# Interleaving the segments of the first two r tiles in the RWKV layer's projections of a two-layer decoder step

## The chip, the cores and the metric

The kernel runs on one core of one Trainium2 chip. The metric is the device time of one execution in microseconds (us), taken on the chip; the median of several runs counts. A profile is one execution of the same program, with every instruction's start and duration on the core's engines: TensorE (PE; its weight loads are shown as PEld), VectorE (DVE), ScalarE (ACT), GpSimd (POOL) and SyncE (SP), which here only issues DMA transfers.

## What is computed

One inference step of a two-layer decoder. Layer 0 is a gated DeltaNet mixer, layer 1 an RWKV-7 mixer. 1104 token rows (64 sample tokens, 16 meta tokens, 1024 prompt tokens) run through both, with D = 1024. The change touches layer 1 only, of which this is the part that matters:

```python
xprev = jnp.concatenate([shift_prev[:, None], xn[:, :-1]], 1)
xx = xprev - xn
xs = xn[None] + xx[None] * mu[:, None, None, :]              # six mixed inputs
rkvz = jnp.einsum('sbtd,sde->sbte', xs[:4], w_rkvz)          # four 1024 x 1024 projections
r, k, v, z = rkvz[0], rkvz[1], rkvz[2], rkvz[3]
w = -jax.nn.softplus(-(w0 + jnp.tanh(xs[4] @ w1) @ w2)) - 0.5
a = jax.nn.sigmoid(a0 + (xs[5] @ a1) @ a2)
kk = l2norm((k * k_k).reshape(B, T, H, N))
decay = jnp.exp(-jnp.exp(w))
# then, token by token: S = S*decay - (S kk)(kk a)^T + v k^T ;  y = S r
```

The recurrence over tokens is computed in blocks of 64 tokens. Each block needs the inverse of a small triangular system, made from k, a and the decay alone; r, v and z are not needed for it.

## The kernel before

Tokens lie along the free dimension, in three segments of 384, 384 and 336 columns (`SEGS`). An output tile is 128 of the 1024 channels of one projection; each of its three segments is a sum of 24 matmuls: 8 pieces of the input dimension, each as high half of the weight times high half of x, low times high, and high times low (`dense_tile`, L1436). x and the weights are split into such halves (`split`, L135): ACT casts the high half (whi, or the high half of xa, xc, xh; L139), and POOL or DVE subtracts to give the low half (wlo, or the low half; L143). The tiles xa, xc, xh and xl hold the eight pieces of x in high and low halves.

In layer 1, `keys_decay_rate` (L1452) first makes k, the decays and a; their PE tiles are d and flora, and their results go to DRAM (kd, csd, ad). After it come the weights' opening (`projection_weights`, L2334), the mixed input of r (`mix`, L1290, with the temporaries mixs, three buffers; by segment, and in a segment piece by piece), and `projections` (L2370): 24 tiles, in the order r (m = 0), v (m = 2), z (m = 3), each with its segments in turn. Each tile's result is copied by ACT from PE's accumulator (d, L2494) and stored (rd for r, L2495).

A weight tile comes in two halves of 256 KB, numbered h: tile ti uses h = 2 ti for its first four pieces of x and 2 ti + 1 for the others. `fetch(h)` issues its load on SP's queue (wraw, two buffers), `cast(h)` splits it (whi and wlo, four buffers each). So a cast of h waits until PE has read the last matmul with h - 4, and a fetch of h until the split of h - 2 is done.

Inside `projections` the order is written by hand: PE's work is counted in half-tiles. After each half-tile (12 matmuls) `gap()` is called, which issues all that the list `plan` holds for that number, on all engines. The casts and fetches have such numbers, worked out from `starts`, the half-tile at which a tile begins. So do the openings of the recurrence's blocks, 24 items, one every three half-tiles: item n is loaded at about half-tile 3n + 1 (sldcs, slda, sldk, on SP) and begins at 3n + 4 (`system_steps`, L1566): on ACT two exponentials and a square (sal, sldcs, sqs), on DVE and POOL products (skk, sal, slda), and on PE the small matmuls frss and fL between half-tiles. Every fifth item is followed by the inverse on DVE (invtmp, invT) of the batch.

The part before `projections` (the opening of the weights, the mixing) is placed by the compiler's scheduler, which weaves it into the engines' queues beside the hand-made order; within one engine the queue is then strict. So mixing of r's x goes on beside the first tiles.

The lines of the loop that the change rewrites:

```python
for ti, (m, k) in enumerate(tiles):
    dst = {0: self.rd, 2: self.vd, 3: self.zd}[m]
    for s, (c0, n) in enumerate(SEGS[0:count(m, k)]):
```

Of the kernel before, what the change touches and what calls it, by code (L numbers as in the profile page):

```python
# [16 lines left out]
SEGS = [(0, 384), (384, 384), (768, 336)]  # L17
# [37 lines left out]
class Stream:  # L55
# [5 lines left out]
    def fetch(self):  # L61
        if self.fetched < len(self.srcs):
            w = self.raw[self.fetched] = self.b.t(self.b.wp, [128, 4, 128], "wraw", 2)
            v = self.srcs[self.fetched]
            m = v.shape[2]
            self.b.nc.sync.dma_start(w.rearrange("p a b -> p (a b)").rearrange("p (k m) -> p k m", m=m), v)
            self.fetched += 1

    def cast(self):
        if self.made < len(self.srcs):  # L70
            hi, lo = (self.b.t(self.b.wp, [128, 4, 128], n, self.b.WB, F32R) for n in ("whi", "wlo"))
            self.b.split(self.raw.pop(self.made), hi, lo)
            m = self.srcs[self.made].shape[2]
            self.w[self.made] = [x.rearrange("p a b -> p (a b)").rearrange("p (k m) -> p k m", m=m) for x in (hi, lo)]
            self.made += 1
# [13 lines left out]
class Builder:  # L89
# [8 lines left out]
    def t(self, pool, shape, tag, bufs=1, dt=F32):  # L98
        self.uid += 1
        return pool.tile(shape, dt, name=f"{tag}_{self.uid}", tag=tag, bufs=bufs)  # L100
# [2233 lines left out]
    def projection_weights(self):  # L2334

        nc, t = self.nc, self.t
        tiles = [(m, k) for m in (0, 2, 3) for k in range(8)]
        raw, whi, wlo = {}, {}, {}

        def fetch(h):  # L2340
            m, k = tiles[h // 2]
            v = self.i["rwkv_w_rkvz"][0, m][:, 128 * k:128 * k + 128].rearrange("(k p) m -> p k m", p=128)
            raw[h] = t(self.wp, [128, 4, 128], "wraw", 2)
            nc.sync.dma_start(raw[h], v[:, 4 * (h % 2):4 * (h % 2) + 4, :])

        def cast(h):
            whi[h], wlo[h] = (t(self.wp, [128, 4, 128], x, self.WB, F32R) for x in ("whi", "wlo"))
            self.split(raw.pop(h), whi[h], wlo[h])
        for h in (0, 1):
            fetch(h)  # L2350
        for h in (0, 1):
            cast(h)
            fetch(h + 2)
        cast(2)
        fetch(4)
        return tiles, whi, wlo, fetch, cast

    def late_weights(self):
# [11 lines left out]
    def projections(self, xa, xb, ip, opened, tiles, whi, wlo, fetch, cast):  # L2370
# [5 lines left out]
        count = lambda m, k: 3 if m == 3 and k >= self.ZK else len(segs[m])  # L2376
        plan = [[] for _ in range(180)]

        def put(g, f, late=2):
            plan[g].append((late, f))  # L2380
# [16 lines left out]
        starts, g = [], 0  # L2397
        for m, k in tiles:
            starts.append(g)
            g += 2 * count(m, k)  # L2400
        for h in range(3, 48):
            g = starts[h // 2]
            if h % 2 == 0:
                put(starts[h // 2 - 1] + 1, lambda h=h: cast(h), 1)
                put(starts[h // 2 - 1] + 3, lambda h=h: h + 2 < 48 and fetch(h + 2), 0)
            else:
                put(max(0, g - 1) if h > 3 else 5, lambda h=h: cast(h), 0)
                put(g + 1 if h > 3 else 7, lambda h=h: h + 2 < 48 and fetch(h + 2), 0)

        for m in (2, 3):  # L2410
            e, p0 = (48, 0) if m == 2 else (96, 48)
# [15 lines left out]
        for n in range(24):  # L2427
            B, g = batches[n // 5], g0(n)
# [12 lines left out]
        for B in batches:  # L2441
            g = g0(B.items[-1]) + 9
# [3 lines left out]
            g = at = max(at + 4, g + 2)  # L2446
# [4 lines left out]
            g = at + 4  # L2451
# [17 lines left out]
        g = starts[-1] + 2 * count(3, 7)  # L2469
# [10 lines left out]
            for x, f_ in sorted(self.plan.pop(at, []), key=lambda x: x[0]):  # L2480
                put(120 + 2 * u, f_, 4)

        for ti, (m, k) in enumerate(tiles):
            dst = {0: self.rd, 2: self.vd, 3: self.zd}[m]
            for s, (c0, n) in enumerate(SEGS[0:count(m, k)]):
                w = Halves(whi, 2 * ti), Halves(wlo, 2 * ti)
                p = self.dense_tile(w, zin if (m, s) == (3, 2) else xs[m], (0 if (m, s) == (3, 2) else c0, n), gap)

                def out(p=p, c0=c0, n=n, m=m, k=k, dst=dst):
                    f = t(self.ev, [128, 384], "ev", 3)  # L2490
                    if m == 3:
                        self.gate(f[:, 0:n], p[:, 0:n])
                    else:
                        nc.scalar.copy(f[:, 0:n], p[:, 0:n])  # L2494
                    put(now[0] + 2, lambda: nc.sync.dma_start(dst[k][:, c0:c0 + n], f[:, 0:n]))  # L2495
                put(now[0], out, 0)
# [130 lines left out]
```

## Time and profile before

| | us |
|---|---|
| median of 3 runs | 2273.2 |
| lowest and highest of them | 2270.88, 2274.19 |
| the profiled execution | 2271.01 |
| span of its trace | 2269.3 |

Times in the trace are counted from the span's start. Layer 1's opening weights (h = 0 on) are fetched from 1402.7 us on, and the stores of r go from 1448.0 to 1587.2 us. How to read the views: the page lists, for the whole execution, each engine's busy time and the chain that ended last, followed backwards from the last instruction to what released it. A timeline lists single instructions with their start, duration and, in brackets, the idle time of the engine ahead of them and what ended it. A window table gives the busy time of each engine in a stretch of the span, the granted clock of PE as a share of the full one, and the share of the DMA engines' time in use.

### The profile page before, as it was taken

The page shows a single profiled execution, that of the slowest core. Times are in us where ns is not written, and L with a number is a line of the kernel's source. Part 1 is how long each engine was busy: PE and PEld are TensorE (multiplying, and loading weights), DVE is VectorE, ACT ScalarE, POOL GpSimd, SP SyncE. Part 2 cuts the span into 40 slices and gives each one's busy share as a digit, 9 for nine tenths or more (in the row PEclk, how much of TensorE's full clock was granted, in tenths as well). Part 3 has the DMA queues.
Part 4 walks back from the last instruction along what each step waited for, and adds up shares of the span by engine and source line. Part 5 has one row for each costly group of instructions (what it writes and reads, how often), then busy time and mean ns, then how long its engine had stood idle before and what let it go on. Part 6 is the DMA issues. An engine that isn't in the chain of part 4 may idle for free.

```text
span 2269.3 us, 55274 instructions
## 1 busy us (share of the span) xinstructions
PE 2143.4 (94%) x20382; PEld 1966.5 (87%) x20382; DVE 1584.5 (70%) x4167; ACT 1250.7 (55%) x3631; POOL 1004.0 (44%) x1385
## 2 busy tenths in 40 slices
PE   7889999999999999989999999898999999999997
PEld 6788889889898989878999999798889977788886
DVE  6778788796969687885435762559887637667765
ACT  5536565556556565645433464644545456676763
POOL 4416262534335252614341442464543345566663
PEclk9999999999999999999999999999999999999997
DMA  3324242424333342436344234577786676655532
GB/s 113 79 67 127 65 124 67 110 80 109 85 105 99 81 122 71 114 78 184 95 143 106 70 103 169 167 237 196 206 247 155 157 186 155 173 162 158 168 118 91
DMA packets 495400, 291.61 MB, mean 129 GB/s; under 512 B 222345, under 2 KB 480506, under 8 KB 495130
## 3 DMA queue, kind: packets, MB, share of 16 engines
q1 hardware_dynamic: 495130, 288.08, 45.2%
q8 instruction: 161, 2.64, 0.5%
q14 instruction: 109, 0.89, 0.1%
HBM read 195.66 MB, written 92.30 MB: 127 GB/s over the span
## 4 chain that ended last, share of the span: by engine, by line
PE 46%; DVE 28%; issue 7%; ACT 6%; DMA 6%; POOL 3%; SPq 3%; DVEq 0%; POOLq 0%; ACTq 0%
PE d L129 10%; DVE invtmp L689 5%; PE rA L133 5%; DVE invT L691 5%; DVE cvy L634 4%; PE dz L129 4%; PE zo L129 3%; PE do L129 3%; PE rA L129 3%; PE dv L129 2%; PE fG L129 2%; PE dk L129 1%; DMA wraw<-in_gdn_w_out 1%; POOL wlo L143 1%; DVE E L765 1%
## 5 line engine op out<-in xcount | busy, mean ns | idle before, releaser
L143 POOL TENSOR_TENSOR wlo<-wraw,whi 128x512 fp32r<-128x512 f32 x238 | 321.1, 1350 | 490.1 <-ACT whi L139 391.5
L634 DVE SCALAR_TENSOR_TENSOR cvy<-raw,cw,cvy 128x408 f32<-128x408 f32 (+2 forms) x288 | 180.0, 625 | 35.8 <-ACT cvy L115 30.5
L689 DVE TENSOR_TENSOR invtmp<-invA,invT 72x31 f32<-72x31 f32 (+31 forms) x403 | 189.0, 469 | 15.6 <-POOL invT L678 10.1
L129 PE MATMUL d<-xc,whi 128*128 128x384 f32 (+1 forms) x640 | 181.4, 344 | 6.7 <-ACT xc L139 2.9
L691 DVE TENSOR_TENSOR invT<-invT,invtmp 72x31 f32<-72x31 f32 (+31 forms) x403 | 176.6, 438 | 14.1 <-DVE invtmp L689 0.2
L115 ACT ACTIVATE raw<-cvy 128x408 f32<-128x408 f32 (+2 forms) x96 | 49.8, 518 | 226.2 <-DVE cvy L634 178.0
L139 ACT CAST whi<-wraw 128x512 fp32r<-128x512 f32 x238 | 145.3, 612 | 26.0 <-DMA wraw<-in_rwkv_w_rkvz 12.5
L129 PE MATMUL dv<-xc,whi 128*128 128x384 f32 (+1 forms) x480 | 154.6, 343 | 0.0
L129 PE MATMUL dz<-xc,whi 128*128 128x384 f32 (+1 forms) x480 | 153.2, 342 | 0.0
L129 PEld LDWEIGHTS d<-xc,whi 128*128 128x128 f32 x640 | 118.0, 191 | 10.5 <-ACT xc L139 3.5
L129 PE MATMUL d<-xc,wlo 128*128 128x384 f32 (+1 forms) x320 | 105.4, 339 | 1.9 <-POOL wlo L143 1.8
L129 PE MATMUL d<-xa,whi 128*128 128x384 f32 (+1 forms) x336 | 101.2, 344 | 3.4 <-ACT whi L139 1.6
L129 PE MATMUL dz<-xa,whi 128*128 128x384 f32 (+1 forms) x288 | 102.3, 355 | 0.7 <-DVE zg L905 0.7
L129 PE MATMUL dv<-xa,whi 128*128 128x384 f32 (+1 forms) x288 | 100.9, 350 | 0.0
L1929 POOL TENSOR_SCALAR y<-y,mv,grs 128x64 f32<-128x64 f32 x132 | 81.1, 632 | 34.7 <-DVE grs L164 29.4
L129 PEld LDWEIGHTS dz<-xc,whi 128*128 128x128 f32 x480 | 90.4, 191 | 0.9
L129 PEld LDWEIGHTS dv<-xc,whi 128*128 128x128 f32 x480 | 89.0, 188 | 2.2 <-issue 1.6
L958 POOL TENSOR_SCALAR Sb<-Sb,eglb 128x128 f32<-128x128 f32 x128 | 90.4, 718 | 0.0
L160 POOL TENSOR_TENSOR ors<-ovar,cvals 128x6 f32<-128x6 f32 x24 | 35.8, 1492 | 118.9 <-DVE ovar L1121 118.6
L129 PE MATMUL d<-xl,whi 128*128 128x384 f32 (+1 forms) x256 | 82.8, 337 | 0.8 <-DVE xl L143 0.8
L129 PE MATMUL d<-xh,whi 128*128 128x384 f32 (+1 forms) x256 | 83.0, 336 | 0.1
L129 PE MATMUL d<-xh,wlo 128*128 128x384 f32 (+1 forms) x256 | 82.5, 336 | 0.0
(543 smaller groups left out, 7154.0 us busy)
## 6 DMA issues: line engine op xcount, KB each, us to landing
wraw<-in_gdn_w_in SPq DMA_DIRECT2D x96, 256.0 KB
wraw<-in_rwkv_w_rkvz SPq DMA_DIRECT2D x74, 256.0 KB
Sb<-in_state_gdn SPq DMA_DIRECT2D x64, 256.0 KB
wraw<-in_rwkv_w_o SPq DMA_DIRECT2D x48, 256.0 KB
E<-drow SPq DMA_DIRECT2D x24, 384.0 KB
attn<-drow SPq DMA_DIRECT2D x24, 384.0 KB
wraw<-in_gdn_w_out SPq DMA_DIRECT2D x36, 256.0 KB
out_s_gdn<-Sb SPq DMA_DIRECT2D x32, 256.0 KB
```

The source lines that it names most:

```text
L115: return self.nc.scalar.activation(out, in_, func, bias=bias, scale=scale, **kw)
L129: self.nc.tensor.matmul(out, lhsT, rhs, start=start, stop=stop)
L133: self.nc.tensor.matmul(out, lhsT, rhs, start=start, stop=True, skip_group_check=True)
L139: nc.scalar.copy(hi, x)
L143: e.tensor_tensor(lo, x, hi.bitcast(F32), op=ALU.subtract)
L160: self.nc.gpsimd.tensor_tensor(y, x, half.broadcast_to(sh), op=ALU.pow)
L634: nc.vector.scalar_tensor_tensor(ys[s][:, 0:wd(s)], raws[s][:, k:k + wd(s)], cw[k], ys[s][:, 0:wd(s)], op0=ALU.mult, op1=ALU.add)
L689: nc.vector.tensor_tensor(tmp, A[:, j, j + 1:32].unsqueeze(2).broadcast_to([nb, n, m]), Tv[:, j, 0:m].unsqueeze(1).broadcast_to([nb, n, m] ...
L691: nc.vector.tensor_tensor(Tv[:, j + 1:32, 0:m], Tv[:, j + 1:32, 0:m], tmp, op=ALU.subtract)
L765: nc.vector.scalar_tensor_tensor(E[:, tt, h], p_[s][:, 128 * tt:128 * tt + 128], c.bp[:, 3 * s + tt, h:h + 1], E[:, tt, h], op0=ALU.mult, ...
L958: nc.gpsimd.tensor_scalar(Sb[g][:, u], Sb[g][:, u], self.eglb[:, hv, 4 * g + u:4 * g + u + 1], None, op0=ALU.mult)
L1929: nc.gpsimd.tensor_scalar(y[:, q], y[:, q], mv[:, q, 0:1], P.rs[:, q:q + 1], op0=ALU.subtract, op1=ALU.mult)
```

## The change

The first two tiles (both of r) run by segments in turn: tile 0 and tile 1 with segment 0, both with segment 1, both with segment 2. From tile 2 on the order is as before. Casts of h = 0 to 3 (four buffers) all stand in the opening, with the fetches up to h = 5. Casts of h = 4 and 5 move from half-tiles 7 and 11 to 8 and 10, their fetches of h = 6 and 7 from 9 and 13 to 10 and 12.

```diff
         for h in (0, 1):
             fetch(h)
-        for h in (0, 1):
+        for h in range(4):
             cast(h)
             fetch(h + 2)
-        cast(2)
-        fetch(4)
         return tiles, whi, wlo, fetch, cast
...
-        for h in range(3, 48):
+        for h, g in ((4, 8), (5, 10)):
+            put(g, lambda h=h: cast(h), 1)
+            put(g + 2, lambda h=h: fetch(h + 2), 0)
+        for h in range(6, 48):
             g = starts[h // 2]
             if h % 2 == 0:
                 put(starts[h // 2 - 1] + 1, lambda h=h: cast(h), 1)
                 put(starts[h // 2 - 1] + 3, lambda h=h: h + 2 < 48 and fetch(h + 2), 0)
             else:
-                put(max(0, g - 1) if h > 3 else 5, lambda h=h: cast(h), 0)
-                put(g + 1 if h > 3 else 7, lambda h=h: h + 2 < 48 and fetch(h + 2), 0)
+                put(g - 1, lambda h=h: cast(h), 0)
+                put(g + 1, lambda h=h: h + 2 < 48 and fetch(h + 2), 0)
...
-        for ti, (m, k) in enumerate(tiles):
+        order = [(ti, s) for s in range(3) for ti in (0, 1)]
+        order += [(ti, s) for ti in range(2, 24) for s in range(count(*tiles[ti]))]
+        for ti, s in order:
+            m, k = tiles[ti]
             dst = {0: self.rd, 2: self.vd, 3: self.zd}[m]
-            for s, (c0, n) in enumerate(SEGS[0:count(m, k)]):
+            for c0, n in SEGS[s:s + 1]:
```

Each tile is numbered when it is made, so most numbers in the change are 6 higher for the same thing (the low-half weights and the mixed x keep their places in the rows). Lines from about L2400 on are 4 higher.

**PE, where tile 0's first segment ends.** whi_18275 and whi_18281 are the two high halves of tile 0's weight in both versions (h = 0 and 1), whi_18287 is that of tile 1 (h = 2). Before:

```order
L129 MATMUL flora_18256<-xa_100,lw2l_17144 128x336
L129 MATMUL d_18444<-xa_100,whi_18281 128x384
L129 MATMUL d_18475<-xa_100,whi_18275 128x384
L129 MATMUL d_18475<-xa_100,wlo_18276 128x384
L129 MATMUL d_18475<-xa_100,whi_18275 128x384 x2
```

In the change:

```order
L129 MATMUL flora_18256<-xa_100,lw2l_17144 128x336
L129 MATMUL d_18450<-xa_100,whi_18281 128x384
L129 MATMUL d_18481<-xa_100,whi_18287 128x384
L129 MATMUL d_18481<-xa_100,wlo_18288 128x384
L129 MATMUL d_18481<-xa_100,whi_18287 128x384 x2
```

The first segment is followed by tile 1's first instead of tile 0's second. Tile 0's third segment (128x336) comes after tile 1's second, d_18554, and after the recurrence's first fL; before, it stood two segments earlier:

```order
L129 MATMUL d_18554<-xa_100,whi_18293 128x384
L129 MATMUL d_18554<-xa_100,wlo_18294 128x384
L129 MATMUL d_18554<-xa_100,whi_18293 128x384
L129 MATMUL fL_18605<-skk_18529,sal_18530 64x64 x12
L129 MATMUL d_18630<-xa_100,whi_18275 128x336
L129 MATMUL d_18630<-xa_100,wlo_18276 128x336
```

**ACT, where the mixing of the third segment meets the recurrence's first item.** mixs rows of 128x336 are the third segment's mixing, casts from them make its pieces; ev<-d rows copy finished PE tiles; sal, sqs and sldcs belong to the items. Before:

```order
L2494 COPY ev_18521<-d_18475 128x384
L115 ACT_TABLE_LOAD
L115 ACTIVATE sal_18524<-sldcs_18469 128x383
L115 ACTIVATE sqs_18525<-sldk_18473,pcol_331 128x384
L139 CAST xc_104<-mixs_18399 128x336
L115 ACTIVATE mixs_18409<-xb_2582_14087,omu_520 128x336
L115 ACTIVATE sldcs_18469<-sldcs_18469 128x384
L139 CAST whi_18547<-wraw_18285 128x512
L139 CAST xc_104<-mixs_18404 128x336
L115 ACTIVATE mixs_18414<-xb_2583_14088,omu_520 128x336
L139 CAST xc_104<-mixs_18409 128x336
L139 CAST xh_2809_15429<-mixs_18414 128x336
```

In the change:

```order
L115 ACTIVATE sldcs_18475<-sldcs_18475 128x384
L115 ACTIVATE mixs_18415<-xb_2582_14087,omu_520 128x336
L139 CAST xc_104<-mixs_18410 128x336
L115 ACTIVATE mixs_18420<-xb_2583_14088,omu_520 128x336
L2498 COPY ev_18567<-d_18508 128x384
L139 CAST xc_104<-mixs_18415 128x336
L115 ACTIVATE sal_18620<-sldcs_18521 128x383
L115 ACTIVATE sqs_18621<-sldk_18525,pcol_331 128x384
L139 CAST xh_2809_15429<-mixs_18420 128x336
```

The cast of the weight half h = 3 (whi<-wraw) is gone from here; a copy of a PE tile (d_18508, tile 0's second segment) and the second item's sal and sqs now stand between the casts of the pieces. The weight's cast is found about 30 rows earlier, ahead of the cast of the first segment's last piece:

```order
L115 ACTIVATE mixs_18375<-xb_2582_14087,omu_520 128x384
L1433 COPY ev_18188<-d_18163 128x384
L139 CAST whi_18293<-wraw_18285 128x512
L139 CAST xa_100<-mixs_18348 128x384
L1433 COPY ev_18216<-d_18191 128x336
```

Before, the same rows stand there without the third.

**POOL, at the same place.** Rows from mixs make low halves of the pieces of x; skk and slda belong to the items. Before:

```order
L1583 TENSOR_TENSOR skk_18523<-skk_18523,sldcs_18469 128x384
L143 TENSOR_TENSOR wlo_18548<-wraw_18285,whi_18547 128x512
L1585 TENSOR_SCALAR slda_18471<-slda_18471,pcol_331,omka_83 128x384
L143 TENSOR_TENSOR xc_104<-mixs_18404,xc_104 128x336
L143 TENSOR_TENSOR xl_2810_15430<-mixs_18414,xh_2809_15429 128x336
L1592 TENSOR_TENSOR slda_18471<-slda_18471,sldk_18473 128x384
L143 TENSOR_TENSOR xa_100<-mixs_18424,xa_100 128x336
```

In the change:

```order
L1583 TENSOR_TENSOR skk_18529<-skk_18529,sldcs_18475 128x384
L1585 TENSOR_SCALAR slda_18477<-slda_18477,pcol_331,omka_83 128x384
L143 TENSOR_TENSOR xc_104<-mixs_18410,xc_104 128x336
L1592 TENSOR_TENSOR slda_18477<-slda_18477,sldk_18479 128x384
L1576 MEMSET sal_18620 128x6
L143 TENSOR_TENSOR xl_2810_15430<-mixs_18420,xh_2809_15429 128x336
L1578 MEMSET sal_18620 128x8
L1583 TENSOR_TENSOR skk_18619<-skk_18619,sldcs_18521 128x384
L143 TENSOR_TENSOR xa_100<-mixs_18430,xa_100 128x336
```

The weight's low half has left this place, the first item's second slda step stands ahead of xl, and the second item's skk ahead of the last piece (xa).

## The prediction

> **What bounds the kernel now.** I read the page's totals first: TensorE (PE) is the busiest engine and the largest share of the chain that ended last.
>
> ```profile
> PE 2143.4 (94%) x20382; PEld 1966.5 (87%) x20382; DVE 1584.5 (70%) x4167; ACT 1250.7 (55%) x3631; POOL 1004.0 (44%) x1385
> PE 46%; DVE 28%; issue 7%; ACT 6%; DMA 6%; POOL 3%; SPq 3%; DVEq 0%; POOLq 0%; ACTq 0%
> ```
>
> Then the stage that the diff touches, cut into stretches at tile edges (start and end in us, then busy us and count of each engine, the granted PE clock, DMA share, GB/s).
>
> ```profile
> core 0: us, PE busy (x) PEld busy (x) DVE busy (x) ACT busy (x) POOL busy (x), PEclk, DMA share, GB/s
> 1443.07:1447.40 4.33, 4.33 (x26) 4.33 (x27) 3.58 (x6) 3.31 (x9) 3.15 (x8) 1.00 0.59 205
> 1447.40:1461.66 14.26, 8.18 (x26) 5.75 (x25) 8.12 (x11) 8.88 (x18) 8.87 (x10) 0.67 0.55 177
> 1461.66:1478.07 16.41, 16.41 (x170) 15.30 (x168) 3.90 (x10) 5.11 (x11) 8.46 (x14) 0.98 0.50 159
> 1478.07:1520.90 42.83, 42.83 (x436) 39.78 (x434) 18.33 (x37) 18.67 (x41) 28.14 (x40) 1.00 0.81 238
> 1520.90:1620.00 99.10, 91.27 (x988) 83.58 (x988) 93.27 (x178) 49.84 (x112) 48.62 (x54) 0.97 0.69 198
> ```
>
> The first row is tile 0's second segment: 4.33 us, no gap. The second row is its third segment. It has fewer columns (336 for 384), yet takes 14.26 us; PE is busy for 8.18 of them, at two thirds of the clock. The third row is the whole of tile 1. The timeline of PE tells why (start, us, instruction, idle time before it and what ended it):
>
> ```profile
> 1442.89 0.62 PE L129 MATMUL d<-xa,whi 128*128 128x384 f32 x2 [0.66 <-POOL xa L143]
> ...
> 1448.30 0.42 PE L129 MATMUL d<-xa,whi 128*128 128x336 f32 x1
> 1451.34 0.42 PE L129 MATMUL d<-xc,whi 128*128 128x336 f32 x1 [2.62 <-ACT xc L139]
> ...
> 1452.21 0.65 PE L129 MATMUL d<-xc,whi 128*128 128x336 f32 x1 [0.29 <-DVE xc L143]
> 1453.11 0.65 PE L129 MATMUL d<-xc,whi 128*128 128x336 f32 x1 [0.25 <-ACT xc L139]
> ...
> 1456.87 0.93 PE L129 MATMUL d<-xc,whi 128*128 128x336 f32 x2 [2.83 <-POOL xc L143]
> ```
>
> The third segment waits for its own input, the mixed x (tiles xa, xc, xh, xl), piece by piece: 2.62 + 0.29 + 0.25 + 2.83 = 5.99 us of idle PE, and the rest at a low clock. The chain of waits confirms that the pieces set the pace here (start, us, what):
>
> ```profile
> 1452.26 1.23 POOL skk L1583
> 1453.49 1.23 POOL wlo L143
> 1454.71 0.93 POOL slda L1585
> 1455.64 0.28 issue
> 1455.93 0.89 POOL xc L143
> 1456.81 1.12 POOL xl L143
> 1457.94 1.23 POOL slda L1592
> 1459.16 0.91 issue
> 1460.12 0.90 POOL xa L143
> 1461.01 0.04 issue
> 1461.06 3.13 PE d L129 x13
> 1464.18 0.79 PE frss L129 x24
> 1464.98 2.29 PE d L129 x12
> 1467.27 0.84 PE fL L129 x24
> ...
> 1473.30 2.04 PE d L129 x12
> 1475.34 0.84 PE fL L129 x24
> 1476.18 4.14 PE d L129 x24
> ```
>
> Up to 1461 the chain lies on POOL (mixing, and the recurrence's skk and slda), after it on PE alone. So the stage waits for x once, and for about ten us.
>
> **The change, part by part.** *The order of the six segments.* Nothing is added or removed on PE; tile 1's first two segments and tile 0's second now stand ahead of tile 0's third. I rebuild PE's path from 1443.07, where tile 0's first segment ends in both versions. Prices: an unbroken 384-column segment 4.33 (first window row). Tile 1's middle segment is broken by the recurrence's matmuls: half of 4.33, frss 0.79, second half 2.29, fL 0.84, together 6.09. A 336-column segment: halves 2.04 and, from 1476.18 to the tile's edge at 1478.07, 1.89, so 3.93. Tile 1's third, with frss and fL: 0.79 + 2.04 + 0.84 + 1.89 = 5.56. Sum 4.33 + 4.33 + 6.09 + 3.93 + 5.56 = 24.2 us. Before, the same work runs from 1443.07 to 1478.07, 35.0 us. **If no piece of x is late, PE gains 10.8 us.** Of this 10.3 are the third segment's 14.26 - 3.93; the rest is the low clock at the head of tile 1.
>
> *Is x in time?* Tile 0's third segment now starts at 1443.07 + 4.33 + 4.33 + 6.09 = 1457.8 instead of 1447.4. It takes the eight pieces one after the other, about 0.49 us each (3.93 / 8), and the last one at about 1461.5. The pieces themselves keep their path, but POOL's queue differs: the low half of the weight (wlo, 1.23) leaves it, the next item's skk (1.23, taken like the first) comes in ahead of the last piece. From 1452.26: skk 1.23, slda 0.93, gap 0.28, xc 0.89 ends at 1455.6, where 1459.5 would do; slda 1.23 and xl 1.12 end at 1457.9, where 1460.8 would do; skk 1.23 and xa 0.90 end at 1460.1, where 1461.5 would do. The least slack is 1.4 us, before what follows.
>
> *The moved weight cast.* The fourth half (h = 3) is now split in the opening, some 16 us earlier on ACT, and so on POOL; the fetches of h = 5 and after move with it on SP's queue.
>
> ```profile
> 1439.20 0.58 ACT L115 ACTIVATE ev<-flora,pcol 128x384 f32<-128x384 f32 x1 [1.04 <-DMA kd<-ev]
> ...
> 1452.08 0.60 ACT L139 CAST whi<-wraw 128x512 fp32r<-128x512 f32 x1
> 1452.59 0.47 ACT L139 CAST xc<-mixs 128x336 fp32r<-128x336 f32 x1
> ```
>
> The cast costs ACT 0.51 (1452.08 to 1452.59). At its new place, about 1436, ACT has 1.04 us of idle time three microseconds later, where it waits for the landing of a kd store that leaves ahead of the cast. That hides it for the piece that tile 0's first segment waits for (1442.89). Without this cover the cost is 0.5. The scans and loads that hang on the ACT instruction between the two may slip by the same 0.5: the last piece then ends at 1460.6, slack 0.9. POOL's 1.23 falls in a stretch with POOL idle. SP waits there for POOL's split before it can refill that buffer; the csd stores stand behind it, but their scans start 1.5 us later anyway. I take nothing for all this, with 0 and 0.5 as ends.
>
> *The later casts.* h = 4 and 5 may be split only when tile 0's third segment has read its halves, at half-tiles 8 and 10. From the first, at about 1459.8, to tile 2's start at 1467.3 there are 7.5 us; cast and split take 0.6 and 1.23, behind at most the last piece. On ACT the eviction of the third segment and the cast of h = 5 stand behind that wait; neither is due before 1461.7. Nothing, unless POOL is 5 us behind.
>
> *SP's queue.* The loads of the recurrence's items now have less lead. Their stores, casts and evictions are the same in number.
>
> ```profile
> 1446.07 0.38 SPq L1554 DMA_DIRECT2D sldk<-kd  x1
> ...
> 1470.89 0.32 SPq L1554 DMA_DIRECT2D sldk<-kd  x1
> 1450.11 0.62 DVE L1580 SCALAR_TENSOR_TENSOR skk<-sldk,pcol,slda 128x384 f32<-128x384 f32 x1 [1.50 <-DMA sldk<-kd]
> ...
> 1481.90 0.62 DVE L1580 SCALAR_TENSOR_TENSOR skk<-sldk,pcol,slda 128x384 f32<-128x384 f32 x1
> ```
>
> The first two loads of 1446 are in use 4.0 us after issue (1450.11, a real wait). The fourth item's, issued at 1470.89, is used 11.0 us later. In the change I find it issued at about 1464.3, behind a weight fetch that waits for POOL's split of h = 4, and used at 1469.5 or later: lead 5.2 against 4.0. I take nothing; the ends are nothing and 2 us.
>
> *What comes after.* From tile 2 on, the order on every engine is the old one, and positions are counted in half-tiles. So all of it moves with PE, if nothing there is tied to another clock. The window from 1520.90 is VectorE's (93.27 of 99.1 us busy), yet the chain enters it from PE:
>
> ```profile
> 1520.93 0.82 PE frss L129 x24
> ...
> 1522.07 1.15 DVE skk L1580
> ```
>
> DVE is idle for more than half of the window before (18.33 of 42.83), so it carries no backlog into it. The gain is kept.
>
> **The sum.** The profiled execution took 2271.01 us; less 10.8 it is 2260.2. The median of the runs is 2273.2, 2.2 above it, so the forecast is **2262.4**.
>
> Two rules of the Trainium skill bear on this. The row at 1447.40 shows a clock of 0.67 around gaps of 2.62 and 2.83 us. The page "TensorE: Matmul & The Clock Gate", section "Part 1: The HAM clock gate", says that PE falls to half rate after an idle window of about 3.4 us, that these windows run free of the program, and that it stays there for at least one; the trace agrees in kind (gaps below 3.4 us were enough here), and by it the loss goes away with the gaps. POOL's slda took 0.93 above. The page "SBUF — State Buffer", section "SBUF: two separate sides", says that a VectorE operation with two SBUF inputs and a GpSimd operation lock each other out for a whole instruction; as the change crowds the same pieces and two items of the recurrence into these microseconds, it speaks against the slack: an estimate by it, one 0.62 us DVE operation ahead of each of three POOL operations, makes the last piece 1.9 us later and the gain about 1 us smaller.
>
> **The rivals.** *A smaller stall remains.* For it: slack of 0.9 to 1.4 us, three engines in strict queues, ACT copies of finished PE tiles now standing between the casts. Against it: the other pieces have 3 us. If the mixing slips by 4 us, PE waits 3, and loses about as much as half of the old clock loss (14.26 - 5.99 - 3.93 = 4.3, so 2): gain 5.8, 2267; by 2 us, 2264.
>
> *The gain is given back.* If the DMA queues (0.81 busy, 238 GB/s from 1478 to 1520) or VectorE after 1520 hold a pace of their own, PE arrives earlier and waits there: 2273. Against it: PE is busy in all of the 42.83 us and VectorE's first steps follow PE.
>
> *The low-clock spells move.* The window from 1520.90 has 0.97 of the clock: 99.1 x 0.03 / 0.5 is 6 us at half, which costs up to 3 us of PE. The gaps that cause it stand, but spells may fall otherwise after a shift: 2259 or 2266. (This is the page on the clock gate again, free-running windows.)
>
> *Slower.* The loads' lead: if a load of sldcs, slda or sldk takes 9 us instead of 4.0 while the weight fetch stands ahead of it, each of the first items holds ACT, and with it the eviction of PE's tiles, by some 4 us. Four items cost 16 us, more than the gain: 2278. It decides from a landing of about 5 us on, if several items are hit; a lead of 11 us returns once POOL has caught up, which speaks against four.
>
> That the change doesn't do what it says is out: PE's order has the third segment behind tile 1's second.
>
> **How the numbers follow.** Forecast 0.64; a smaller stall 0.14; given back 0.10; spells 0.06; slower 0.05; 0.01 is left. A measurement of this kernel can tell about 0.2% (4.5 us) from no change. Faster by more: forecast, smaller stall and spells, 0.84. Same: given back and the rest, 0.11. Slower 0.05. The range goes from the spells' good end, with a little for the edges, 2258.5, to the smaller stall's bad end, 2267.5.
>
> **What would show it.** Right: PE's row for tile 0's third segment without idle time, at about 1458 to 1462, 4 us long, clock near 1.00 in the whole stretch; tile 2 starting near 1467; the chain on PE from 1443 on, POOL's pieces gone from it; the windows after it as long as before. A smaller stall would show as "<-POOL xa" or "<-POOL xl" ahead of d near 1460. Given back: tile 2 early, but tile 8 or the end not. Slower: PE ahead of frss or fL waiting for sqs, skk, and ACT for sldk. The forecast is wrong if tile 2 starts after 1471, or if the end moves by less than tile 2 does.

## The result, and the profile after

| | before | the change |
|---|---|---|
| median, us | 2272.8 (4 runs) | 2259.3 (4 runs) |
| lowest and highest, us | 2270.88, 2274.19 | 2256.02, 2262.72 |
| profiled execution, us | 2271.01 | 2262.07 |
| span of its trace, us | 2269.3 | 2260.3 |

The ratio of the times is 0.994, with a 95% interval of 0.9922 to 0.9958: faster by 0.4 to 0.8%. The forecast was 2262.4 in a range from 2258.5 to 2267.5. The medians lie 13.5 us apart, more than the 10.8 that were forecast and than the 10.1 that the stage itself gives below. The interval (9.5 to 17.7 us) holds all three figures, and the two repeats give 11.5 and 12.1; whether some 2 us come from elsewhere, the runs do not show. All medians in this document leave out two executions that took far longer than the others of their kernel, 3993.51 us of the kernel before and 2864.16 us of a variant.

The page of the change, first the engines' busy times, then the shares of the chain that ended last:

```profile
PE 2142.3 (95%) x20382; PEld 1967.9 (87%) x20382; DVE 1581.5 (70%) x4167; ACT 1251.0 (55%) x3631; POOL 1005.7 (44%) x1385
PE 51%; DVE 26%; ACT 7%; issue 6%; DMA 6%; POOL 3%; SPq 1%; DVEq 0%; POOLq 0%; ACTq 0%
```

PE does the same matmuls (20382). Its share of the chain rose from 46% to 51%, that of the issue of DMAs on SP fell from 3% to 1%; these are totals of the whole span, and the windows of the stage say more. They are cut where the segments end, so each of the first five rows is one segment of the new order: tile 1's first, tile 0's second, tile 1's second (with frss and fL), tile 0's third, tile 1's third (with frss and fL). Columns as before.

```profile
1444.40:1448.74 4.34, 4.34 (x26) 4.34 (x27) 3.58 (x6) 3.32 (x9) 3.16 (x8) 1.00 0.63 210
1448.74:1453.10 4.36, 4.36 (x27) 4.36 (x26) 1.79 (x3) 4.07 (x8) 1.04 (x3) 1.00 0.78 237
1453.10:1459.00 5.90, 5.90 (x73) 5.33 (x71) 4.63 (x9) 5.11 (x12) 5.50 (x6) 1.00 0.40 136
1459.00:1463.67 4.67, 4.33 (x28) 3.70 (x25) 3.67 (x6) 1.85 (x4) 2.73 (x5) 1.00 0.61 211
1463.67:1469.30 5.63, 5.63 (x73) 5.35 (x73) 2.33 (x4) 2.30 (x5) 5.33 (x8) 1.00 0.59 164
1469.30:1512.40 43.10, 43.10 (x444) 40.06 (x444) 19.77 (x40) 18.86 (x42) 29.61 (x42) 1.00 0.90 265
1512.40:1611.40 99.00, 91.34 (x985) 83.65 (x983) 93.21 (x178) 49.95 (x113) 48.88 (x54) 0.97 0.69 197
```

The first five add up to 24.9 us, where the same matmuls took 35.0 before. PE is busy in all but 0.34 us of them, and the granted clock is 1.00 throughout. The third segment fell from 14.26 us at 0.67 of the clock to 4.67 us. The sixth and seventh row, 43.10 and 99.00 us, are what they were (42.83 and 99.10): the frss near which they are cut starts 42.79 us after tile 2 in both traces (1478.07 to 1520.86, and 1469.30 to 1512.09).

PE's timeline shows the one wait left, and that it stands where the prediction looked for it (start, us, instruction, idle before it and what ended that):

```profile
1444.22 0.62 PE L129 MATMUL d<-xa,whi 128*128 128x384 f32 x2 [0.78 <-POOL xa L143]
...
1463.32 0.42 PE L129 MATMUL d<-xa,whi 128*128 128x336 f32 x1 [0.34 <-POOL xa L143]
```

Between 1444.22 and 1463.32 no row of PE names a wait, frss at 1455.07 and fL at 1458.15 among them; at 1463.32 it waits 0.34 us for the last piece. The chain of waits around it (start, us, what):

```profile
1459.40 0.62 DVE skk L1580
1460.06 0.09 issue
1460.15 1.26 POOL skk L1583
1461.41 0.91 issue
1462.36 0.92 POOL xa L143
1463.28 0.04 issue
1463.32 0.42 PE d L129
1463.74 0.79 PE frss L129 x24
```

So the chain still runs through x up to 1463, though PE waits only 0.34 us for it. After that PE alone carries the chain through the stage.

Is the gain kept? One window from tile 2's first matmul to the end of the span, first of before, then of the change (this one begins 0.1 us behind tile 2's first matmul, which is at 1469.30):

```profile
1478.07:2269.30 791.23, 751.18 (x9626) 665.47 (x9624) 551.01 (x1463) 445.71 (x1276) 416.69 (x518) 0.97 0.62 172
```

```profile
1469.40:2260.30 790.90, 750.58 (x9625) 665.22 (x9623) 550.62 (x1465) 446.13 (x1276) 418.27 (x520) 0.97 0.62 173
```

From 1469.30 on it is 791.0 us, against 791.23 before: all of the gain reaches the end. The two spans differ by 9.0 us: 10.1 less from the end of tile 0's first segment to tile 2 (35.0 to 24.9), 0.2 less behind it, and 1.3 more ahead of it (1443.07 to 1444.40), where both kernels run the same matmuls.

### The profile page after: what moved, and what is told of

It is laid out like the page before. It is cut to its first block, busy times and chain, and to the rows that moved or that the text cites. A ratio compares the mean times of both kernels' runs of the same rounds, so it can differ in the third digit from the quotient of the medians.

```text
span 2260.3 us, 55274 instructions
## 1 busy us (share of the span) xinstructions
PE 2142.3 (95%) x20382; PEld 1967.9 (87%) x20382; DVE 1581.5 (70%) x4167; ACT 1251.0 (55%) x3631; POOL 1005.7 (44%) x1385
## 4 chain that ended last, share of the span: by engine, by line
PE 51%; DVE 26%; ACT 7%; issue 6%; DMA 6%; POOL 3%; SPq 1%; DVEq 0%; POOLq 0%; ACTq 0%
PE d L129 12%; PE rA L133 5%; PE dz L129 4%; PE do L129 4%; DVE invtmp L689 4%; DVE cvy L634 4%; DVE invT L691 4%; PE rA L129 3%; PE zo L129 3%; PE dv L129 3%; PE fG L129 2%; PE dk L129 2%; DMA wraw<-in_gdn_w_out 1%; PE zz L129 1%; DVE E L765 1%
## 5 line engine op out<-in xcount | busy, mean ns | idle before, releaser
L691 DVE TENSOR_TENSOR invT<-invT,invtmp 72x31 f32<-72x31 f32 (+31 forms) x403 | 176.9, 439 | 14.1 <-DVE invtmp L689 0.2
L139 ACT CAST whi<-wraw 128x512 fp32r<-128x512 f32 x238 | 145.4, 612 | 29.5 <-DMA wraw<-in_rwkv_w_rkvz 14.1
```

The lines of the kernel that those rows point to most:

```text
L139: nc.scalar.copy(hi, x)
L691: nc.vector.tensor_tensor(Tv[:, j + 1:32, 0:m], Tv[:, j + 1:32, 0:m], tmp, op=ALU.subtract)
```

## The experiments

The measure below is the time from the end of tile 0's first segment to tile 2's first matmul, the same work on PE in all kernels with these edges: 35.0 us before, 24.9 in the change. Its edges are good to some 0.2 us. The runs with one execution show the measure and the waits in one trace; their times alone could not tell a few us, as single executions of the kernel before went from 2264 to 2283. In four stretches of measurement the kernel before had medians of 2272.4, 2270.5, 2274.1 and 2270.5.

### The change again

No edit. It ran twice more, the second time beside a later experiment.

> The change once more, for its spread. My theory (tile 0's third segment waited for the pieces of its mixed x, and gets other PE work ahead of it now): tile 0's third segment lasts 4 to 5 us, tile 2 starts 10 us earlier after tile 0's first segment than before (25 instead of 35 us), and the rest follows unchanged, so the time is 9 to 14 us under the kernel before. The rival, that part of the 13.5 us between the medians comes from elsewhere than this stage: the traces differ by more than 2 us in a part that the change doesn't touch.

> The change again, unedited, to stand beside the run with the last piece on VectorE. Theory: 2257 to 2262, 0.4 to 0.7% below the kernel before; tile 2 starts 25 to 26 us after tile 0's first segment ends.

Medians 2260.98 (9 runs) and 2262.01 (6), ratios 0.9944 (0.9926 to 0.9963) and 0.9954 (0.9936 to 0.9972). The windows, first of one, then of the other, with their part behind tile 2:

```profile
1438.42:1463.97 25.55, 25.55 (x217) 24.49 (x218) 15.72 (x26) 16.73 (x36) 17.80 (x27) 0.94 0.56 179
1463.97:2259.40 795.43, 756.39 (x9626) 670.50 (x9624) 552.04 (x1465) 446.87 (x1276) 419.49 (x520) 0.96 0.62 173
```

```profile
1441.00:1465.33 24.33, 24.33 (x218) 23.22 (x219) 16.03 (x26) 16.55 (x36) 17.91 (x27) 1.00 0.61 192
1465.33:2257.40 792.07, 753.42 (x9625) 667.83 (x9623) 551.42 (x1465) 445.89 (x1276) 417.19 (x520) 0.97 0.62 173
```

In both PE is busy for the whole stretch: the 0.34 us wait is not in every execution. 24.33 is the predicted sum of 24.2 within 0.1, and below the 25 to 26 expected of the second repeat; the other lost 1.2 to a low clock (0.94). Both medians are as expected. Behind tile 2 the same program took 791.0, 792.1 and 795.4 us, with granted clocks of 0.97, 0.97 and 0.96: the clock's spells, as far as these traces show, move the time by some 4 us from one execution to the next. Ahead of the stage, too, the traces of one program lie up to 6 us apart (the first segment ends at 1444.4, 1438.4 and 1441.0). So the difference of more than 2 us in parts that the change does not touch, which the rival named, is there, but between executions of one program.

### Only the casts early

```diff
-        for h in (0, 1):
+        for h in range(4):
             cast(h)
             fetch(h + 2)
-        cast(2)
-        fetch(4)
```

The cast of h = 3 and the fetch of h = 5 leave the plan for it (half-tiles 5 and 7). The rest is the kernel before, with the old order of segments.

> The earlier casts alone, with the segments in the old order. My theory: the stall stays; at best the piece on POOL that PE waits for longest comes 1.2 us earlier, as the weight's low half has left the queue ahead of it. From the end of tile 0's first segment to tile 2's start 33.5 to 35 us (35.0 before, 24.9 with the change). The rival, that freeing POOL and ACT of the weight's split is the larger part of the gain: under 29 us.

Time 2269.91 (one run); the measure is 33.5 us. PE's timeline in the third segment:

```profile
1450.73 0.42 PE L129 MATMUL d<-xc,whi 128*128 128x336 f32 x1 [2.36 <-ACT xc L139]
1451.98 0.65 PE L129 MATMUL d<-xc,whi 128*128 128x336 f32 x1 [0.21 <-ACT xc L139]
1454.80 0.93 PE L129 MATMUL d<-xc,whi 128*128 128x336 f32 x2 [1.89 <-POOL xc L143]
1457.15 0.65 PE L129 MATMUL d<-xl,whi 128*128 128x336 f32 x1 [0.30 <-POOL xl L143]
```

The stall stays, 4.8 us of waits for 6.0. The early casts alone give 1.5 us, as the theory had it: the gain needs the order of the segments.

### Only the order, with the fourth cast late

```diff
-        for h in range(4):
+        for h in range(3):
             cast(h)
             fetch(h + 2)
...
-        for h, g in ((4, 8), (5, 10)):
+        for h, g in ((3, 2), (4, 8), (5, 10)):
```

> The change, with one part of it taken back: the cast of h = 3 is issued after half-tile 2 instead of in the opening, so the first segments of the two tiles run in turn while the fourth half of the weights is split beside them. Theory (the gain is PE's order of segments; where the cast of h = 3 stands is worth about its own 0.5 us on ACT and 1.2 us on POOL): tile 2 starts 25 to 27 us after tile 0's first segment ends (24.9 in the change, 35.0 before), with a wait of PE of at most 1.5 us for whi or wlo in tile 1's first segment. Rival (the opening's early casts are what makes the order possible): PE waits 3 us or more in tile 1's first segment, or the pieces of x end so much later that tile 2 starts 29 us or more after that point.

Time 2263.06 (one run); the measure is 28.6 us, between the two expectations: the wait, 0.23 + 2.21 us, is more than the theory allowed and less than the rival asked. POOL's timeline, and then PE's:

```profile
1441.57 1.60 POOL L143 TENSOR_TENSOR wlo<-wraw,whi 128x512 fp32r<-128x512 f32 x1
```

```profile
1440.58 0.44 PE L129 MATMUL d<-xc,whi 128*128 128x384 f32 x1 [0.23 <-ACT whi L139]
1443.22 0.44 PE L129 MATMUL d<-xc,wlo 128*128 128x384 f32 x1 [2.21 <-POOL wlo L143]
...
1444.43 0.52 PE L129 MATMUL d<-xh,wlo 128*128 128x384 f32 x1
1444.75 0.52 PE L129 MATMUL d<-xl,whi 128*128 128x384 f32 x1
...
1447.85 0.33 PE L129 MATMUL d<-xc,whi 128*128 128x384 f32 x1
```

The split of the weight stands on POOL behind other work and is late. 1.2 us after PE goes on, its matmuls stand 0.32 us apart instead of 0.17, for 3.42 us (1444.43 to 1447.85), which costs half of it, some 1.6 us. Waits 2.4 and clock 1.6 less the 0.34 of the change make the 3.7 us (28.6 - 24.9). So the early fourth cast is worth 3.7 us of the 10 between these two traces (3.1 and 4.3 against the two repeats of the change): it is part of the gain and not only a cost. The Trainium skill, "TensorE: Matmul & The Clock Gate", section "Part 1: The HAM clock gate", gives 3.4 us as the length of the gate's window; the spell of 3.42 agrees. The page asks for an idle window of that length ahead of the fall, but the longest gap here was only 2.21; the measurement decides.

### One segment later instead of two

```diff
-        order = [(ti, s) for s in range(3) for ti in (0, 1)]
+        order = [(0, 0), (1, 0), (0, 1), (0, 2), (1, 1), (1, 2)]
```

In the change, with the cast of h = 4 at half-tile 7 and its fetch of h = 6 at 9.

> Half of the change's order: tile 0's third segment gets one segment of tile 1 ahead of it instead of two. My theory: the pieces come at their old time, so the work ahead (4.3 us) is gained and no more: the third segment still waits some 5 us, and tile 2 starts 29 to 31 us after the end of tile 0's first segment. The rival, that the pieces move with the work on PE because of the recurrence's instructions between them in the queues: either the full gain (25 us) or nearly none (34 us).

Time 2267.0 (one run); the measure is 32.3, worse than expected. PE's timeline:

```profile
1457.57 0.42 PE L129 MATMUL d<-xc,whi 128*128 128x336 f32 x1 [1.75 <-POOL xc L143]
...
1460.44 0.51 PE L129 MATMUL d<-xh,whi 128*128 128x336 f32 x1 [0.36 <-ACT xh L139]
1462.71 0.65 PE L129 MATMUL d<-xl,whi 128*128 128x336 f32 x1 [1.47 <-DVE xl L143]
1464.12 1.55 PE L129 MATMUL fL<-skk,sal 64*64 64x64 f32 x24
```

One segment of delay (4.33) leaves 3.6 us of waits, where the theory had 5, and a low clock behind them (fL 1.55 for 0.91). A low clock lay at the head as well: from 1443.93 to 1446.98 the matmuls stand 0.32 us apart. The work is 24.2 and the waits are 3.6, so some 4.5 of the 32.3 are low clock: the waits were fewer than expected, the low clock was more, and the size was missed by 1 to 3 us. The direction is that of the theory: the later the third segment, the less it waits. But the pieces did not all come at their old time. Counted from the end of tile 0's first segment, the fourth piece was ready after 13.2 us, before 13.8; the seventh after 18.3, before 15.2. On ScalarE a weight's cast and the second item's sal and sqs stood ahead of its high half (xh at 1459.93), and on VectorE that item's skk (1460.19, 1.34 us) ahead of its low half (1461.46, 1.19 us). So for the last pieces the rival's mechanism is at work: they move back with PE, because instructions that follow PE's order stand ahead of them in the queues.

### PE kept busy in the old stall

```diff
+            if fill and q in fill:
+                junk = self.ps("m", 2, "fill")
+                for _ in range(fill[q]):
+                    self.mm(junk[:, 0:384], his[0][:, 0], x[0][0][:, 0:384])
```

In `dense_tile` of the kernel before, only in tile 0's third segment: twice 14 added matmuls (2.62 us each time), with nothing read from them.

> The kernel before, with 14 extra matmuls (2.4 us each time) on data that is there, ahead of the third and of the fourth piece of tile 0's third segment, into an unused accumulator: PE is kept busy in most of the stall, so that the low clock should not come. The pieces set the pace (my theory): the segment still ends when its last piece comes, about 14 us after its start; only the head of tile 1 runs faster, 0.5 to 1 us in all. The rival, that the low clock is a loss of its own beside the waits (14.26 - 5.99 - 3.93 = 4.3 us, as the prediction's count had it): the segment lasts about 10 us.

Time 2269.96 (one run). The windows: the third segment, then tile 1.

```profile
1445.60:1459.90 14.30, 10.72 (x55) 8.81 (x54) 8.14 (x11) 9.04 (x19) 8.89 (x10) 1.00 0.55 176
1459.90:1478.66 18.76, 18.76 (x167) 17.45 (x167) 3.90 (x10) 4.96 (x11) 8.37 (x14) 0.82 0.43 140
```

At the full clock and with 5.2 us more work, the segment took 14.30 us instead of 14.26, and the last piece was ready 13.7 us after its start (1459.25), before 13.6 (1461.00). The pieces set its length; the low clock in it had cost nothing by itself. But tile 1, expected to be 0.5 to 1 us faster, ran at 0.82 and took 18.76 instead of 16.41: a spell of low clock now lay where PE is the bound, and there it cost 2.35 us. That it is the same spell, moved, is not shown.

### What made the pieces late

Three edits of the kernel before, each with the old order. All low halves of the third segment on VectorE:

```diff
-                self.mix_part(m, k, c0, c0 + n, xb[k], *xs[k], self.ev)
+                x = self.mix_raw(m, k, c0, c0 + n, xb[k], self.ev)
+                self.split(x, xs[k][0][:, c0:c0 + n], xs[k][1][:, c0:c0 + n], eng_lo="pool" if k % 2 and c0 < 768 else "dve")
```

> The kernel before, in its old order of segments, with one edit: in the third segment of r's mixed input the low halves of all eight pieces are subtracted on VectorE, instead of those of the odd pieces on GpSimd. It takes three or four subtractions of about 0.9 to 1.1 us out of GpSimd's queue, beside the recurrence's skk and slda (1.2 us each). Theory (before, GpSimd's queue sets the pace of the pieces): the third segment shrinks from 14.26 us to 8 to 11 us, and the time falls by 3 to 6 us. Rival (the pieces are paced by ScalarE's strict queue and VectorE's wait for the landing of sldk, GpSimd being only the last in the row): the segment stays at 13 us or more, the time within 1.5 us.

The recurrence's first item one half-tile later:

```diff
-        g0 = lambda n: 3 * n + 4 + (8 if n > 12 else 0)
+        g0 = lambda n: 3 * n + 4 + (8 if n > 12 else 0) + (1 if n == 0 else 0)
```

> The kernel before, in its old order of segments, with the recurrence's first item begun one half-tile later (its load as well). On ScalarE the item's table load, exponential and square still stand ahead of the first xc cast, but the following casts of xc, and on GpSimd the low half of xc, now stand ahead of the item's skk and slda. Theory (before, the pieces of x were late because the first item's instructions stood among them in the strict queues of ScalarE, VectorE and GpSimd, no one engine alone): the first wait for xc stays at 2 to 3.5 us, the later waits (2.83 us for xc on GpSimd) fall below 1.5 us together, and tile 2 starts 31 to 33.5 us after tile 0's first segment ends (35.2 before). Rival (the mixing itself, with its three buffers, cannot go faster): waits of 5 to 6 us in sum again and tile 2 at 34.5 us or more.

Four mixs buffers instead of three, here and in a second place (L2316) where later inputs are mixed:

```diff
-        x = self.t(pool, [128, 384], "mixs", 3)[:, 0:b - a]
+        x = self.t(pool, [128, 384], "mixs", 4)[:, 0:b - a]
```

> The kernel before with four instead of three mixs buffers for the temporaries of the mixing, wherever they are used; the order of segments is the old one. The scheduler weaves the mixing differently with it. Theory (three buffers set the pace of the pieces: the next mixing on ScalarE waits until the oldest piece has its low half, so one slow low half delays the following pieces): PE's waits in tile 0's third segment fall from 6 us to below 3.5 us, and tile 2 starts 29 to 33 us after tile 0's first segment ends (35.2 before). Rival (the pace is the sum of ScalarE's and VectorE's own work, the recurrence's first item among it): waits of 5 us or more, tile 2 at 34 us or more.

PE's timelines in the third segment, with the low halves on VectorE, then with the later item, then with four buffers:

```profile
1451.86 0.43 PE L129 MATMUL d<-xc,whi 128*128 128x336 f32 x1 [3.36 <-ACT xc L139]
1456.15 0.65 PE L129 MATMUL d<-xh,whi 128*128 128x336 f32 x1 [1.32 <-ACT xh L139]
1458.08 0.65 PE L129 MATMUL d<-xl,whi 128*128 128x336 f32 x1 [1.00 <-DVE xl L143]
```

```profile
1451.56 0.42 PE L129 MATMUL d<-xc,whi 128*128 128x336 f32 x1 [3.14 <-ACT xc L139]
1455.53 0.65 PE L129 MATMUL d<-xc,whi 128*128 128x336 f32 x1 [1.49 <-ACT xc L139]
1457.35 0.65 PE L129 MATMUL d<-xc,whi 128*128 128x336 f32 x1 [0.90 <-DVE xc L143]
```

```profile
1451.83 0.42 PE L129 MATMUL d<-xh,whi 128*128 128x336 f32 x1 [0.60 <-ACT xh L139]
```

Waits of 5.7 and 5.5 us for 6.0 in the first two (times 2271.08 and 2270.66, one run each, measures 34.3 and 34.7): the second rival held, the first nearly (from first matmul to first matmul the third segment took 12.8 us, 14.1 before, where the rival asked for 13 and the theory for 8 to 11). Neither GpSimd's queue nor the place of the item on GpSimd set the pace: with the later item GpSimd began the fourth piece's low half at 1452.42 instead of 1455.93, and PE then waited for other rows. With four buffers the waits shrank to 0.60 us and the time was 2262.5 (one run). There the scheduler also wove the work ahead differently, so the measure doesn't apply; from one flora matmul ahead of all that (at 1416.43 before, 1417.90 in the change and 1415.58 here) to tile 2 it is 54.0 us, against 61.6 before and 51.4 in the change. ScalarE's timeline shows how, first before, then with four buffers:

```profile
1448.60 1.28 ACT L115 ACT_TABLE_LOAD   x1
...
1450.83 0.46 ACT L139 CAST xc<-mixs 128x336 fp32r<-128x336 f32 x1
```

```profile
1445.61 1.20 ACT L139 CAST xc<-mixs 128x336 fp32r<-128x336 f32 x3
...
1449.60 1.28 ACT L115 ACT_TABLE_LOAD   x1
```

Before, the first xc cast of the segment stands behind the first item's table load, sal and sqs; with a fourth buffer three such casts stand ahead of it. So with three buffers the mixing did not run ahead of the recurrence's opening. That a mixing waits until an older piece has its low half can be seen in the run with one segment later, where ScalarE's mixs at 1457.55 waits 1.00 us for GpSimd's xc. That the fourth buffer removes most of the stall is shown, in one execution; how much of this is the buffer itself and how much the new weave is not separated.

### Two candidates to beat both

The change with four mixs buffers, and the change with the last piece's low halves on VectorE (`eng_lo="pool" if k % 2 and k < 7 else "dve"` in `mix`); the latter ran twice.

> The change with four instead of three mixs buffers, a candidate to lie below both kernels. In the region the change has left only 0.3 us of wait in the third segment, so at most 0.5 us are to be had there; elsewhere, layer 1's opening also mixes through these buffers, where the scheduler may gain or lose. Theory: the time of the change within 3 us, 2257 to 2264, and tile 2 at 24 to 26 us after tile 0's first segment ends. Rival (the reordered opening matters): more than 3 us above or below the change.

> The change, with one more edit: the low half of the last piece of r's mixed input is subtracted on VectorE in all three segments, instead of on GpSimd, because the wait that is left in the change's tile 0, third segment, is for that row on GpSimd (0.34 us), and the one at the head of the first segment too (0.78 us). Theory (these waits are GpSimd's queue): no wait for xa in the third segment, the wait in the first below 0.4 us, and 0.3 to 1.0 us less than the change over the region; in the whole time that is 0.01 to 0.05%, below what five rounds tell. Rival (the waits come from the mixing ahead of GpSimd): the same waits, now for xa from VectorE, and the time of the change or some tenths of a us more.

> The change with the last piece's low halves on VectorE once more, beside the change itself in the same stretch of measurements. Theory (the edit gives nothing in the region, and the 0.28% by which it stood behind the change lay in a stretch ahead of the edit, with a lower clock, where both kernels hold the same instructions, so it is not the edit's): the medians of the two lie within 2.5 us. Rival (the edit itself costs it): it is again 2.5 us or more above the change, 2263 to 2265 against 2259 to 2261.

| | median, us (runs) | ratio to before, 95% interval |
|---|---|---|
| four buffers | 2264.27 (12) | 0.9971 (0.9957 to 0.9985) |
| last piece on VectorE | 2263.9 (12) | 0.9972 (0.9958 to 0.9986) |
| the same again | 2267.42 (9) | 0.9964 (0.9951 to 0.9977) |

Neither beats the change (0.994, 0.9944, 0.9954). With four buffers the profiled execution had no wait in tile 0's third segment, and the time came out just above the expected 2257 to 2264; tile 2 came 26.7 us after the first segment's end, not 24 to 26, with some flora matmuls and a granted clock of 0.91 in between. On VectorE the first segment's wait grew from 0.78 to 1.83 and 1.80 us, for xa, now from DVE, the third's stayed at 0.33, for ScalarE's cast of xa, and a new one came up at the first frss, 0.41 and 0.60 us for ScalarE's sqs. So PE's waits there are 2.6 and 2.7 us instead of 1.1: the theory of the first run failed, and its rival, the same waits, fell short. In the second pair the ratios lie 0.1% apart and the medians 5.4 us, against the 2.5 expected, so by the medians the rival held; the intervals of the ratios overlap in both pairs. Whether these two are really slower than the change by some 0.2% stays open; of the last piece's variant the traces show some 1.5 us of it, the rest has no cause shown.

## Why the prediction was right, step by step

**The sum.** Predicted 4.33 + 4.33 + 6.09 + 3.93 + 5.56 = 24.2, measured 4.34 + 4.36 + 5.90 + 4.67 + 5.63 = 24.9 in the first trace, and 24.33 in the one without wait or low clock. The gain was 10.1 for 10.8. The term that was too small is the third segment: 3.93, with 4.33 of busy PE and 0.34 of wait in place of it. That the median, 2259.3, lies 3.1 us below the forecast is no merit of the sum, which was 0.7 us too hopeful; it lies within the scatter of the executions (2256.0 to 2262.7).

**The last piece.** "xa 0.90 ends at 1460.1": this was the step that failed, though PE hid most of it. The rows of the change, VectorE's, then ScalarE's, then POOL's timeline:

```profile
1454.90 0.56 DVE L1351 SCALAR_TENSOR_TENSOR mixs<-xb,pcol,mixs 128x336 f32<-128x336 f32 x1
...
1459.40 0.61 DVE L1580 SCALAR_TENSOR_TENSOR skk<-sldk,pcol,slda 128x384 f32<-128x384 f32 x1
1459.93 0.61 DVE L1581 SCALAR_TENSOR_TENSOR sal<-sldk,pcol,sal 128x384 f32<-128x384 f32 x1
1460.46 1.32 DVE L1351 SCALAR_TENSOR_TENSOR mixs<-xb,pcol,mixs 128x336 f32<-128x336 f32 x1
```

```profile
1461.81 0.47 ACT L139 CAST xa<-mixs 128x336 fp32r<-128x336 f32 x1 [1.45 <-DVE mixs L1351]
```

```profile
1460.15 1.26 POOL L1583 TENSOR_TENSOR skk<-skk,sldcs 128x384 f32<-128x384 f32 x1 [0.99 <-DVE skk L1580]
1462.36 0.91 POOL L143 TENSOR_TENSOR xa<-mixs,xa 128x336 fp32r<-128x336 f32 x1 [0.95 <-ACT xa L139]
```

The last piece ends at 1463.27. Less the 1.33 us by which this trace runs late, that is 1461.9, where 1460.1 was predicted and 1461.0 stood before. I had walked POOL's queue alone, where taking wlo out brings the piece forward. For the two pieces ahead of it that came out: xc and xl ended at 1455.6 and 1457.8 by the old count, where 1455.6 and 1457.9 were predicted. (The slda of 0.93 in that count is the chain's cut of a row of 1.24; the gap of 0.28 beside it makes up for that.) But for the last one POOL waits for ScalarE's cast, and that for VectorE's mixs. It did so before the change too: the 0.91 of issue ahead of xa in the prediction's own chain is that wait, so an emptier POOL could not bring the piece forward (0.9 of the 1.8). And on VectorE the next item's skk and sal (0.61 each) now come first: 0.9 later than before. The slack of 0.9 to 1.4 us was used up by it. The seventh piece, whose low half VectorE makes, was only just in time as well: it was ready at 1462.20, and PE took it at 1462.25. The rule of the Trainium skill about VectorE and GpSimd ("SBUF — State Buffer", section "SBUF: two separate sides") put the last piece 1.9 us later by another way. That the size (1.8) agrees is chance, as the lateness came from the two causes above. The way is seen in part: mixs took 1.32 us beside POOL's skk, yet it had taken as long before the change (1.30 at 1458.22); and where it took 0.56, at 1454.90, POOL's slda beside it was the long one (1454.61, 1.23 us, for 0.66 with VectorE idle at 1469.11 before).

**What bounded the kernel before.** That the pieces set the pace was right (the filler shows it). That the chain lay on POOL was true of the view, but POOL was only the last in the row: taking work from it gave 0.7 us. And "the rest at a low clock" was no loss of its own: at the full clock the segment was as long.

**The moved cast.** Its 0.5 us on ScalarE were hidden as predicted: from the flora matmul at 1416.43 (1417.90 in the change) to the end of tile 0's first segment it is 26.6 us before and 26.5 in the change, and ScalarE's wait for the kd store shrank from 1.04 to 0.26. That it also carries 3.7 us of the gain was not in the prediction, which treated it as a cost only.

**The loads.** The fourth item's lead fell from 11.0 to 6.2 us (issued at 1466.72, used at 1472.90), where 5.2 was foreseen, and the landing was longer than the price of 4.0 (the sldk load that ScalarE and VectorE waited for took 4.6 us), yet PE waited for no frss or fL in the stretch: "slower" did not come. "Given back" did not come either: 791.2 and 791.0 us from tile 2 on. **The spells** move by some 4 us between executions of one program, a little more than that rival had it, and with no side; the three medians, 2259.3 to 2262.0, contain this.

## What to carry to other kernels

When an engine waits for inputs that several others make, give it other ready work first, and count what must be ready for that other work: here the order was worth 10 us only with the weights split early (3.7 of them, in one trace). Walk every queue that a late piece passes, not only the one that the chain names last. And before reordering, ask how many temporaries there are: a fourth buffer, with the new weave that came with it, took away most of the same stall.

## What the runs showed of the hardware

A spell of half clock can lie behind the stall instead of in it: with the late cast it began 1.2 us after the wait and was 3.42 us long, after single gaps of at most 2.21 us; with fillers in the stall one came in tile 1 and cost 2.35 us, though PE had been busy for 10.72 of 14.30 us. What decides whether a spell comes is not shown: after a wait of 0.67 us at the head of the stage the matmuls ran at half clock in one repeat of the change and with one segment later, and at the full clock with the late cast. A mixs row of one shape takes 0.56 or 1.32 us, the longer beside GpSimd's skk of 1.26 us; beside the shorter, GpSimd's slda was long (1.23 us for 0.66).
